# Two more MLP pairs by seven products, other low parts by adding transfers, and a new place for the scaled activations in a two-layer decoder trunk

## The chip, the cores and the metric

The kernel runs on one core of a Trainium2 chip. The metric is the device time of one execution in microseconds. Three runs of the kernel before took 1472.92, 1473.97 and 1474.12 us (median 1473.97). The engines are named as in the profile: PE is TensorE's matmul, PEld its weight load, DVE is VectorE, ACT is ScalarE, POOL is GpSimd, SP is SyncE, which here only issues transfers.

## The reference

A hybrid decoder trunk of two layers on one sequence of 512 positions with 1024 features, all float32. Layer 0 mixes with a gated short convolution and differential attention, layer 1 with stick-breaking attention. Each layer then attends into 256 memory tokens and applies a gated MLP of width 2816 with a causal convolution of width 3:

```python
def conv_ffn(h, w_up, w_conv, w_down):
    u = causal_dwconv(h @ w_up, w_conv)
    gate, val = jnp.split(u, 2, axis=-1)
    return (jax.nn.silu(gate) * val) @ w_down

for l in range(DEPTH):
    ...
    x = x + conv_ffn(rmsnorm(x, norm_ffn[l]), ffn_w_up[l], ffn_conv[l], ffn_w_down[l])
```

The change touches these two MLPs: `h @ w_up`, which has 1024 x 5632 weights in each layer.

## The kernel before

**Number format.** Every operand of a matmul is carried as two parts, a rounded one (`hi`) and the rest (`lo`), and every product is three matmuls: hi by hi, hi by lo, lo by hi. ScalarE casts the high part of a weight tile, VectorE subtracts it from the tile to get the low part (`lo<-raw,hi` in the profile). Weights come in tiles of 128 x 1024 (`raw`), by SP's queue, into three buffers; there are five buffers each for high and low parts.

**The up projection in pairs.** The 44 blocks of 128 output columns are worked on as 22 pairs, a gate block and its value block; the order of pairs and of the down projection's groups is the list `FFN_ORDER`. Pair j's weights are the group `Uj_l` of layer l. A pair is computed in one of two ways.

*Ordinary* (`lin_stream`): eight blocks of the contraction by two output blocks by three matmuls, 48 matmuls of 512 columns, two accumulators out of three. Pairs below `UP_SCALED` multiply by the activations before the normalization's factor per position (`N["A"]`, only the gains are in), and the factor is applied when the accumulator is evicted (`c<-acc,rrow`). Pairs from `UP_SCALED` on use scaled activations (`N["S"]`).

*Seven products* (`lin_halved`): the pair's matrix product is cut into two by two blocks (the two output blocks, even and odd blocks of the contraction, and the two halves of the positions) and made from seven products of blocks instead of eight. Each is 4 blocks x 3 matmuls of 256 columns, 84 in all. It needs sums of blocks on both sides. On the activations' side these are made once per MLP by `fold` out of the scaled activations, with their high and low parts (`N["S"]`, `N["T"]`, in tiles `y`, `h`, `kl`, `pt`, `so`, `rrow`), and no product of such a pair starts before `N["folded"]` allows. The results are put together by a copy and seven additions of 256 columns on ScalarE and VectorE.

On the weights' side the sums are made in DRAM (`sums_in_dram`): once the group named in `SUMMED` has produced its first output, SP's queue copies the four blocks (1 MB), and POOL's queue issues three adding transfers, one of 512 KB and two of 256 KB, each waiting for the one before it. `halved_loads` then loads three tiles of 1024 columns ("a", "b", "c") and one of 512 ("d"); each is cast on ScalarE and subtracted on VectorE.

**Low parts by an adding transfer.** For groups in `LOW`, VectorE does nothing. ScalarE writes the negated high part into the low tile, and an adding transfer of 512 KB, issued by POOL, adds the weights from DRAM:

```python
yield act(hi, raw)
if gi in LOW:
    yield act(lo, raw, scale=-1.0)
    yield add_dma(lo, wts[FIRST[gi] + s])
else:
    yield tt(lo, raw, hi.v().f32(), ALU.subtract)
```

**What sets the order.** The whole program is written out in advance by a planner (`Issue.run`). Every piece of work is a stream that asks for one operation at a time; the planner knows a cost for each, takes the engine whose next operation could start first, and among those that could start within a small tolerance takes the lowest priority number. The engines then work through their queues in that order. The numbers that matter: norm chunks 0.5, norm sums `SUM`, the sums of seven products 0.9, evictions 1.0, attention's blocks from 2.0 on, preparing weights 3.0, and additions in DRAM 6.0. `fold` has the priority `FOLD`. Where two streams of the same engine are ready, a smaller number goes first; a stream that waits on another engine is passed.

**Places.** Work buffers of 512 columns (`c`) are six; `fold` uses two for each of its four steps, an eviction one until its convolution is done. The lines that the profile names are helpers: L439 and L442 ScalarE copies and activations, L454 two-tensor operations on VectorE, L462 its three-operand ones (convolution, scaling), L492 matmuls, L501 transfers by SP, L508 adding transfers by POOL. The normalization's row of factors is the tile `rrow`.

Of the kernel before, what the change touches and what calls it, by code (L numbers as in the profile page):

```python
# [34 lines left out]

UP_SCALED = 6
FFN_ORDER = [('u', 0), ('u', 1), ('u', 2), ('u', 3), ('u', 4), ('u', 5), ('u', 6), ('u', 7), ('d', 0, 0), ('u', 8), ('d', 0, 1), ('u', 9), ('u', 10), ('d', 0, 2), ('u', 11), ('u', 12), ('d', 0, 3), ('u', 13), ('u', 14), ('u', 15), ('u', 16), ('d', 1, 0), ('u', 17), ('d', 1, 1), ('u', 18), ('d', 1, 2), ('u', 19), ('u', 20), ('d', 1, 3), ('u', 21), ('d', 2, 0), ('d', 2, 1)]
SEVEN = {0: (7, 8, 9, 10, 11, 12, 13, 14, 15, 16, 17, 18, 19, 20, 21), 1: (7, 8, 9, 10, 11, 12, 13, 14, 15, 16, 17, 18, 19, 20, 21)}  # L40

SUMMED = {0: {7: 'A1', 8: 'A1', 9: 'A2', 10: 'A2', 11: 'EO0', 12: 'EO0', 13: 'EO1', 14: 'KV1_0', 15: 'KV3_0', 16: 'Q0_0', 17: 'Q0_0', 18: 'Q1_0', 19: 'XO0_0', 20: 'XO0_0', 21: 'XO1_0'}, 1: {7: 'U17_0', 8: 'U19_0', 9: 'U21_0', 10: 'SQK0', 11: 'SQK0', 12: 'SV0', 13: 'SQK1', 14: 'SQK2', 15: 'SV1', 16: 'SQK3', 17: 'Q0_1', 18: 'Q1_1', 19: 'XO0_1', 20: 'XO1_1', 21: 'U1_1'}}


def weight_groups():
# [57 lines left out]
GROUPS = weight_groups()  # L103
GN = {g[0]: i for i, g in enumerate(GROUPS)}

LOW = {GN[n] for n in ('U2_0', 'U2_1', 'U3_0', 'U3_1', 'U4_0', 'U4_1', 'U5_0', 'U5_1', 'U6_0', 'U6_1')}
LOW7 = {GN[n] for n in ()}
ADDED = {GN[f"U{j}_{l}"]: GN[after] for l in SUMMED for j, after in SUMMED[l].items()}
HALVED = {GN[f"U{j}_{l}"] for l in SEVEN for j in SEVEN[l]}
NSLOT = [len(g[3]) * len(g[4]) * P // SLOT for g in GROUPS]  # L110
# [37 lines left out]

POW_WAIT = 0.0

PREP_FIRST, SUM_FIRST, SUM = 0.45, 3.2, 1.5

FOLD = 1.4

SUMS = 6.0
PE_RATE, PE_FIX = 2400.0, 0.0133
# [88 lines left out]
class Issue:  # L245
# [8 lines left out]
    def spawn(self, gen, prio):  # L254
        self.seq += 1
        self.streams.append(Stream(gen, prio, self.seq))
# [75 lines left out]
    @staticmethod  # L332
    def free(*ts):
        for t in ts:
            t.pool.idle.append(max(max(w + LAT.get(e, 0.0) for w, e in t.w), max(t.r)))
# [54 lines left out]
def trunk(ctx: ExitStack, tc: tile.TileContext, xT: bass.AP, memT: bass.AP, wts: bass.AP, par: bass.AP, outT: bass.AP):  # L390
# [36 lines left out]
    def act(out, in_, func=AF.Copy, scale=1.0, bias=None, accum=None):  # L427
        out, in_ = vw(out), vw(in_)
        scale, bias, accum = vw(scale), vw(bias), vw(accum)
        d = (0.051 if in_.psum() else 0.093) + in_.n() / 1200.0  # L430
        d += 0.093 * (isinstance(scale, V) + (bias is not None)) + 0.2 * (accum is not None)
        kw = {}
        if bias is not None:
            kw["bias"] = _raw(bias)
        if accum is not None:
            kw["accum_out"] = _raw(accum)
        if func == AF.Copy and scale is not None and not isinstance(scale, V) and scale == 1.0:
            def fn():
                return nc.scalar.copy(out=out.ap, in_=in_.ap)  # L439
        else:  # L440
            def fn():
                return nc.scalar.activation(out=out.ap, in_=in_.ap, func=func, scale=_raw(scale), **kw)  # L442
        return Op("ACT", d, [in_, scale, bias], [out, accum], fn)
# [299 lines left out]
    def prep(groups):  # L743
        for gi in groups:
# [3 lines left out]
            for s in range(NSLOT[gi]):  # L748
# [9 lines left out]
                else:  # L758
                    yield Until(lambda: (gi, s) in raws)
                    raw = raws[gi, s]  # L760
# [3 lines that stand above are left out]
# [114 lines left out]
    def lin(name, kind, A, done, nblk=None):  # L878
        gi = GN[name]
        c = len(GROUPS[gi][4]) * P  # L880
        nm_ = len(GROUPS[gi][4]) if kind == "f" else nblk
        for ki in range(len(GROUPS[gi][3])):
            for m in range(nm_):
                s = (ki * c + (m * P if kind == "f" else 0)) // SLOT
                uses[gi, s] = uses.get((gi, s), 0) + 1
        for m in range(nm_):
            ps = yield AL(aSC if (name, m) in (("V", 3), ("QK0", 0)) else aACC)
            lin_seq[0] += 1
            spawn(lin_stream(gi, m, kind, A, ps, done, c), 10.0 + lin_seq[0] * 1e-3)

    def lin_done(*names):

        def f():
            for n in names:
                gi = GN[n]
                if fin.get(gi, 0) < nm_of[n]:
                    return False
            return True
        return Until(f)
# [80 lines left out]
    def hs_free(N):  # L980
        for h, l in N["A"].values():
            free(h, l)
# [480 lines left out]
    def ffn(l, xin, xout, last):  # L1463
# [40 lines left out]
        def up_done(j):  # L1504
            def done(m, ps):
                gate = m % 2 == 0
                u = ps
                if j < UP_SCALED:
                    u = yield AL(pC)
                    yield Until(lambda: "rrow" in N)  # L1510
                    yield tt(u, ps, N["rrow"], ALU.mult)
                    free(ps)
                t = yield AL(pG)
                yield from conv3(u, f"ffn_conv{l}", j if gate else 22 + j, 44, t)
                free(u)
                if gate:
                    yield act(t, t, AF.Silu)
                    gate_t[j] = t
                    F["silu", l] = F.get(("silu", l), 0) + 1
                else:  # L1520
                    yield Until(lambda: j in gate_t)
                    yield tt(t, t, gate_t[j], ALU.mult)
                    free(gate_t[j])
                    if 4 <= j < 16 or j > 19:
                        q = pHS if j < 16 else pG
                        hi, lo = yield [AL(q, F32R), AL(q, F32R)]
                        o, w = (hi, lo), (hi, lo)
                    else:
                        y = yield AL(pH, F32R, (P, 2, S))
                        o, w = (y[:, 0, :], y[:, 1, :]), (y,)  # L1530
                    yield from split(o[0], o[1], t)
                    free(t)
                    own[j] = w
                    acts[j] = o
            return done

        def up(j):
            done = up_done(j)
            if j in SEVEN[l]:
                acc = yield AL(aACC)  # L1540
# [3 lines left out]
            scaled = Lazy(lambda k: N.get("S", {}).get(k))  # L1544
            yield from lin(f"U{j}_{l}", "f", scaled if j >= UP_SCALED else N["A"], done)

# [29 lines left out]
        def nfree():  # L1576
            yield lin_done(*(f"U{j}_{l}" for j in range(UP_SCALED)))
            hs_free(N)
            yield lin_done(*(f"U{j}_{l}" for j in range(UP_SCALED, 22)))
            free(*N["own"])  # L1580
            yield Until(lambda: 21 in acts)
            free(N["r"], N["rrow"])
        spawn(nfree(), 0.1)

        spawn(fold(), FOLD)
        for step in FFN_ORDER:
# [283 lines left out]
```

## Time and profile before

| | us |
|---|---|
| median of three runs | 1473.97 |
| the profiled execution | 1473.73 |
| its span | 1471.9 |
| TensorE busy | 1465.0 |
| VectorE busy | 1113.1 |
| ScalarE busy | 810.7 |
| POOL busy | 168.5 |

The granted clock was 1.0. The span is about: 0 to 345 the first mixer and memory attention, up to 375 its output projection, 375 to 690 the first MLP, 690 to 861 stick-breaking attention, up to 1120 its output projection and the second memory attention, then the second MLP to the end.

How to read the rows: of a row of instructions in order of time the first number is its start from the span's begin, the second its length, both in us; "out<-in" are the program's tiles; in brackets stands how long the engine had been idle before it and what ended that. A matmul's length is longer than its distance to the next, since matmuls are pipelined. A group row has the count behind x, then busy us, mean ns of one, and idle time before them.

### The profile page before, as it was taken

To read this page: it belongs to the slowest core of one execution; us is meant where nothing else is said; L and a number is where in the kernel's file an instruction comes from. 1 tells how busy PE (TensorE), PEld (TensorE's weight loads), DVE (VectorE), ACT (ScalarE), POOL (GpSimd) and SP (SyncE) were. 2 spreads that over 40 slices of the span, in tenths; PEclk is the share of its full clock that TensorE was granted. 3 is DMA by queue.
4 is the path that set the end of the run, shared out by engine and by line. 5 is a ranking of instruction groups with operands and counts; after the bars stand their busy time and mean duration, and the time that the engine had idled before them with its cause. 6 is when DMAs were issued, how large, how long until landed. Compare 5 with 4: busy or idle time off the path is not lost.

```text
span 1471.9 us, 21459 instructions
## 1 busy us (share of the span) xinstructions
PE 1465.0 (100%) x8048; PEld 1272.2 (86%) x8048; DVE 1113.1 (76%) x1891; ACT 810.7 (55%) x1335; POOL 168.5 (11%) x249
## 2 busy tenths in 40 slices
PE   9999999999999999999999999999999999999998
PEld 8888888888889999999888888888888889999897
DVE  7689766665798788867687989967656996888683
ACT  6576546453675445444477877855535854545341
POOL 3212121211210000000111111001101300000000
PEclk9999999999999999999999999999999999999999
DMA  6128898967784445658465463453547954455351
GB/s 237 58 86 243 224 264 269 255 169 161 178 177 143 144 151 170 200 169 227 158 154 147 122 187 79 137 178 107 148 126 219 224 149 128 144 159 184 117 165 57
DMA packets 86088, 243.41 MB, mean 165 GB/s; under 512 B 8064, under 2 KB 8576, under 8 KB 85504
## 3 DMA queue, kind: packets, MB, share of 16 engines
q1 hardware_dynamic: 63744, 200.09, 40.2%
q0 software_dynamic: 22240, 41.95, 17.6%
q8 instruction: 63, 1.03, 0.3%
q14 instruction: 41, 0.34, 0.1%
HBM read 239.91 MB, written 65.01 MB: 207 GB/s over the span
## 4 chain that ended last, share of the span: by engine, by line
PE 95%; DVE 2%; ACT 2%; DMA 1%; issue 1%; SPq 0%; DVEq 0%; ACTq 0%
PE acc L492 67%; PE sc L492 13%; PE pv L492 6%; PE tr L492 6%; PE tr L496 3%; DVE lo L454 0%; ACT h L439 0%; DMA raw<-wts 0%; ACT g L442 0%; DMA x<-xT 0%; DVE g L1619 0%; DVE h L454 0%; DVE g L454 0%; DVE c L454 0%; ACT pt L439 0%
## 5 line engine op out<-in xcount | busy, mean ns | idle before, releaser
L492 PE MATMUL acc<-hs,hi 128*128 128x512 f32 x1568 | 493.7, 392 | 0.0
L439 ACT CAST hi<-raw 128x1024 fp32r<-128x1024 f32 (+1 forms) x294 | 303.3, 1038 | 211.1 <-PE acc L492 79.8
L454 DVE TENSOR_TENSOR lo<-raw,hi 128x1024 fp32r<-128x1024 f32 (+1 forms) x274 | 328.7, 1205 | 90.7 <-ACT hi L439 89.5
L492 PEld LDWEIGHTS acc<-hs,hi 128*128 128x128 f32 x1568 | 292.4, 188 | 57.7
L492 PE MATMUL acc<-hs,lo 128*128 128x512 f32 x784 | 307.5, 392 | 0.0
L492 PE MATMUL acc<-hi,hs 128*128 128x512 f32 x544 | 175.4, 395 | 0.3 <-ACT hs L442 0.3
L492 PEld LDWEIGHTS acc<-hs,lo 128*128 128x128 f32 x784 | 147.3, 188 | 28.7
L492 PE MATMUL acc<-h,hi 128*128 128x512 f32 (+1 forms) x600 | 170.2, 368 | 0.0
L454 DVE TENSOR_TENSOR x<-x,acc 128x512 f32<-128x512 f32 (+1 forms) x105 | 71.2, 680 | 71.4 <-PE acc L492 71.1
L492 PEld LDWEIGHTS acc<-h,hi 128*128 128x128 f32 x600 | 108.2, 189 | 18.1
L462 DVE SCALAR_TENSOR_TENSOR g<-c,pp,g 128x511 f32<-128x511 f32 (+1 forms) x168 | 116.9, 745 | 2.5 <-ACT g L442 2.4
L492 PEld LDWEIGHTS acc<-hi,hs 128*128 128x128 f32 x544 | 100.9, 188 | 20.3 <-ACT hs L442 0.6
L492 PE MATMUL acc<-h,lo 128*128 128x512 f32 (+1 forms) x300 | 109.5, 368 | 0.0
L492 PE MATMUL acc<-lo,hs 128*128 128x512 f32 x272 | 106.8, 393 | 0.0
L492 PE MATMUL acc<-y,hi 128*128 128x512 f32 (+1 forms) x280 | 74.2, 346 | 0.0
L508 POOL DMA_DIRECT2D dr<-wts x30 | 27.4, 913 | 392.1 <-DMA dr<-wts 385.6
L442 ACT ACTIVATE g<-c,pp 128x512 f32<-128x512 f32 x84 | 58.1, 719 | 19.1 <-DVE c L454 18.9
L454 DVE TENSOR_TENSOR g<-g,g 128x512 f32<-128x512 f32 (+2 forms) x112 | 62.9, 568 | 5.0 <-ACT g L439 2.0
L492 PEld LDWEIGHTS acc<-h,lo 128*128 128x128 f32 x300 | 56.6, 189 | 9.4
L442 ACT ACTIVATE g<-sc,rq 128x128 f32<-128x128 f32 (+7 forms) x128 | 61.2, 537 | 5.4 <-PE sc L492 4.9
L508 POOL DMA_DIRECT2D dr<-dr x60 | 50.3, 848 | 115.3 <-DMA dr<-wts 70.1
L492 PEld LDWEIGHTS acc<-lo,hs 128*128 128x128 f32 x272 | 51.2, 188 | 10.0
(241 smaller groups left out, 2672.1 us busy)
## 6 DMA issues: line engine op xcount, KB each, us to landing
raw<-wts SPq DMA_DIRECT2D x226, 512.0 KB, 4.2
raw<-dr SPq DMA_DIRECT2D x60, 512.0 KB, 3.7
dr<-wts POOLq DMA_DIRECT2D x30, 512.0 KB, 6.1
dr<-dr POOLq DMA_DIRECT2D x60, 256.0 KB, 4.7
lo<-wts POOLq DMA_DIRECT2D x20, 512.0 KB, 7.8
raw<-wts SPq DMA_DIRECT2D x38, 256.0 KB, 3.1
x<-xT SPq DMA_DIRECT2D x16, 256.0 KB, 4.7
raw<-memT SPq DMA_DIRECT2D x4, 512.0 KB, 4.5
```

Of the source, the lines that this page charges most:

```text
L439: return nc.scalar.copy(out=out.ap, in_=in_.ap)
L442: return nc.scalar.activation(out=out.ap, in_=in_.ap, func=func, scale=_raw(scale), **kw)
L454: lambda: _ve(eng).tensor_tensor(out=out.ap, in0=in0.ap, in1=in1.ap, op=op))
L462: lambda: nc.vector.scalar_tensor_tensor(out=out.ap, in0=in0.ap, scalar=_raw(scalar), in1=in1.ap, op0=op0, op1=op1))
L492: lambda: nc.tensor.matmul(out.ap, lhsT.ap, rhs.ap, start=start, stop=stop))
L496: return Op("PE", 0.109, [in_, ident_v], [out], lambda: nc.tensor.transpose(out.ap, in_.ap, ident_v.ap))
L508: lambda: nc.gpsimd.dma_start(out=out.ap, in_=i, accum_op=ALU.add, max_dma_last_dim=2048))
```

## The change

Pairs 5 and 6 of both MLPs go from ordinary to seven products, and pair 5 no longer gets the factor at eviction, since it uses the scaled activations. The groups with low parts by an adding transfer were pairs 2 to 6 and are pairs 1 to 4. The additions in DRAM are 34 instead of 30, and the groups after which they are made are new: in layer 0 most come earlier by one or two groups and four come after pairs 7 to 10 of the MLP itself; ten of layer 1's come during layer 0's MLP, none in stick-breaking attention's projections, and four after pairs 8 to 11 of layer 1's MLP. `fold` gets priority 0.8, which is ahead of evictions (1.0) instead of behind them, and the norm sums 0.7 instead of 1.5.

```diff
-UP_SCALED = 6
+UP_SCALED = 5
-SEVEN = {0: (7, 8, 9, 10, 11, 12, 13, 14, 15, 16, 17, 18, 19, 20, 21), 1: (7, 8, 9, 10, 11, 12, 13, 14, 15, 16, 17, 18, 19, 20, 21)}
-
-SUMMED = {0: {7: 'A1', 8: 'A1', 9: 'A2', 10: 'A2', 11: 'EO0', 12: 'EO0', 13: 'EO1', 14: 'KV1_0', 15: 'KV3_0', 16: 'Q0_0', 17: 'Q0_0', 18: 'Q1_0', 19: 'XO0_0', 20: 'XO0_0', 21: 'XO1_0'}, 1: {7: 'U17_0', 8: 'U19_0', 9: 'U21_0', 10: 'SQK0', 11: 'SQK0', 12: 'SV0', 13: 'SQK1', 14: 'SQK2', 15: 'SV1', 16: 'SQK3', 17: 'Q0_1', 18: 'Q1_1', 19: 'XO0_1', 20: 'XO1_1', 21: 'U1_1'}}
+SEVEN = {0: (5, 6, 7, 8, 9, 10, 11, 12, 13, 14, 15, 16, 17, 18, 19, 20, 21), 1: (5, 6, 7, 8, 9, 10, 11, 12, 13, 14, 15, 16, 17, 18, 19, 20, 21)}
+
+SUMMED = {0: {5: 'A0', 6: 'A1', 7: 'A1', 8: 'A2', 9: 'A2', 10: 'EO0', 11: 'EO0', 12: 'EO1', 13: 'KV1_0', 14: 'Q0_0', 15: 'Q0_0', 16: 'Q1_0', 17: 'XO0_0', 18: 'U7_0', 19: 'U8_0', 20: 'U9_0', 21: 'U10_0'}, 1: {5: 'U9_0', 6: 'U11_0', 7: 'U12_0', 8: 'U13_0', 9: 'U14_0', 10: 'U15_0', 11: 'U16_0', 12: 'U17_0', 13: 'U18_0', 14: 'U20_0', 15: 'Q0_1', 16: 'Q1_1', 17: 'XO0_1', 18: 'U8_1', 19: 'U9_1', 20: 'U10_1', 21: 'U11_1'}}
...
-LOW = {GN[n] for n in ('U2_0', 'U2_1', 'U3_0', 'U3_1', 'U4_0', 'U4_1', 'U5_0', 'U5_1', 'U6_0', 'U6_1')}
+LOW = {GN[n] for n in ('U1_0', 'U1_1', 'U2_0', 'U2_1', 'U3_0', 'U3_1', 'U4_0', 'U4_1')}
...
-PREP_FIRST, SUM_FIRST, SUM = 0.45, 3.2, 1.5
-
-FOLD = 1.4
+PREP_FIRST, SUM_FIRST, SUM = 0.45, 3.2, 0.7
+
+FOLD = 0.8
```

## The prediction

> **What bounds the kernel now.** I read the page first: busy times, then the chain that ended last.
>
> ```profile
> span 1471.9 us, 21459 instructions
> PE 1465.0 (100%) x8048; PEld 1272.2 (86%) x8048; DVE 1113.1 (76%) x1891; ACT 810.7 (55%) x1335; POOL 168.5 (11%) x249
> ...
> PE 95%; DVE 2%; ACT 2%; DMA 1%; issue 1%; SPq 0%; DVEq 0%; ACTq 0%
> ```
>
> TensorE holds 95% of the chain: fewer or shorter matmuls are worth their full time, as long as nothing makes TensorE wait. Next the chain in order of time, which shows TensorE's pace in the gated MLP, and windows (columns: PE, PEld, DVE, ACT and POOL busy with counts, granted clock, DMA share, GB/s) over the first MLP's start, its rest, three seven-product pairs in a row, and the stick-breaking layer.
>
> ```profile
> 461.50 12.34 PE acc L492 x60
> 473.84 1.44 PE sc L492 x12
> ...
> 389.50:452.00 62.50, 62.50 (x281) 51.85 (x280) 58.19 (x95) 44.99 (x63) 8.42 (x7) 1.00 0.77 177
> 452.00:690.00 238.00, 238.00 (x1642) 222.80 (x1641) 185.05 (x282) 111.31 (x149) 5.09 (x6) 1.00 0.56 173
> 560.00:590.00 30.00, 30.00 (x252) 30.00 (x251) 28.66 (x48) 18.63 (x26) 0.00 (x0) 1.00 0.58 180
> 690.00:861.00 171.00, 169.99 (x840) 141.50 (x839) 141.23 (x228) 118.86 (x224) 28.14 (x76) 1.00 0.57 151
> ```
>
> In the MLP TensorE never stops. VectorE is the engine behind it: 58.19 of 62.50 us (93%) in the first seven pairs, when the scaled activations are made, and 28.66 of 30 (96%) over three seven-product pairs in a row, still without a TensorE gap.
>
> **The gain on TensorE.** Twelve 256-column matmuls take 1.44 us, 0.120 each, so a seven-product pair (7 x 4 x 3 = 84) takes 10.08 us. The x60 piece is 48 matmuls of 512 columns and the first twelve of the next pair: 12.34 - 1.44 = 10.90 us for 48, which is also what an ordinary pair has (8 x 2 x 3). One pair converted saves 0.82 us. Pairs 5 and 6 of two MLPs are four: -3.28 us.
>
> A rule of the Trainium skill speaks against this (TensorE: Matmul & The Clock Gate, "Back-to-back issue gap"): in a stream of weight loads and matmuls it gives 131 ns a matmul at 512 columns and 81 at 128. An estimate between the two by columns is 98 ns at 256: 8.2 us for the 84 against 6.3 for the 48, a loss of 1.9 per pair and 7.8 in all. The rows decide: 0.120 and 0.227 here.
>
> **What moves onto VectorE, and when.** Four moments in the first MLP (groups over 389.4 to 452, then instructions in order of time):
>
> ```profile
> L462 DVE SCALAR_TENSOR_TENSOR g<-c,pp,g 128x511 f32<-128x511 f32 (+1 forms) x24 | 17.5, 744 | 1.2 <-ACT g L442 1.2
> L454 DVE TENSOR_TENSOR c<-acc,rrow 128x512 f32<-128x512 f32 x12 | 8.1, 685 | 5.0 <-ACT rrow L439 3.6 <-PE acc L492 1.5
> L454 DVE TENSOR_TENSOR c<-c,c 128x256 f32<-128x256 f32 x8 | 3.3, 418 | 0.0
> ...
> 389.49 1.29 DVE L454 TENSOR_TENSOR c<-acc,rrow 128x512 f32<-128x512 f32 x2 [3.55 <-ACT rrow L439]
> 390.70 0.74 DVE L462 SCALAR_TENSOR_TENSOR c<-x,pp,rrow 128x512 f32<-128x512 f32 x1
> ...
> 431.11 1.22 DVE L454 TENSOR_TENSOR lo<-raw,hi 128x1024 fp32r<-128x1024 f32 x1
> 432.24 0.75 DVE L462 SCALAR_TENSOR_TENSOR g<-c,pp,g 128x511 f32<-128x511 f32 x1
> 432.91 0.68 DVE L454 TENSOR_TENSOR pt<-c,pt 128x512 fp32r<-128x512 f32 x1
> ...
> 449.68 0.68 DVE L454 TENSOR_TENSOR rrow<-c,pt 128x512 fp32r<-128x512 f32 x1
> 450.28 1.22 DVE L454 TENSOR_TENSOR lo<-raw,hi 128x1024 fp32r<-128x1024 f32 x1
> ...
> 451.27 0.40 PE L492 MATMUL acc<-y,hi 128*128 128x256 f32 x2
> ```
>
> At 389.5 the row of norm factors exists and VectorE's rush begins. The last part of the scaled activations ends at 450.3, and pair 7, the first of seven products, starts at 451.27: just in time. Starts one after another give what an operation occupies: 0.60 us for 512 columns (two in 1.21), 0.67 for the convolution's (432.24 to 432.91), 1.13 for a low part of 1024; 0.42 stands for 256. So the scaled activations take 8 x 0.67 + 16 x 0.60 + 16 x 0.42 = 21.7 us; evicting an ordinary scaled pair 2 x (0.60 + 2 x 0.67) + 2 x 0.60 = 5.1; the weights of a seven-product pair 3 x 1.13 + 0.60 = 4.0.
>
> Pair 0 started 7 x 10.90 us before 451.27, at 375.0, so pair 5 is due at 429.5. Its sixth product, which wants its last weights, is due 5 x 1.44 = 7.2 us later, at 436.7. Before, the same point of pair 7 is at 458.5: 69.0 us after 389.5, for 21.7 + 6 x 5.1 + 3.9 (pair 6, unscaled, 5.1 - 1.2) + 4.0 = 60.2 us of work; 9 us spare. After: 47.2 us for 21.7 + 5 x 5.1 + 4.0 = 51.2. Four us too much, if every eviction of pairs 0 to 4 must come before pair 5's weights. None needs to: TensorE wants their buffers, which the first 0.60 us of each half frees. What must be done by 436.7 is 21.7 + 4.0 + 10 x 0.60 and enough convolutions that the six work buffers don't run out. But the weights have the lowest claim on VectorE (3.0 against 1.0 for evictions); they pass only where no eviction is ready. The low part at 431.11 is such a passing, with the scaled activations (1.4) still unfinished. At 429.5 the backlog is 21.7 + 25.5 - 40.0 = 7.2 us, with some 2.5 halves under way, each often waiting for ScalarE. I take no stall (they pass), and as bounds 0 and strictly last: 7.2 + 1.1 = 8.3 us per MLP.
>
> That the scaled activations come first has a price at 389.5: their first two operations (1.34 us) go ahead of the eviction that frees an accumulator for pair 1's second half, due at 375.0 + 3 x 5.45 = 391.35. The eviction would end at 389.5 + 1.34 + 0.6 = 391.4, and the signal comes on top: 0.2 us per MLP, +0.4 (bounds 0 and 2 x 1.3).
>
> **Low parts by adding transfer.** Pairs 5 and 6 had theirs from the transfer and get them from VectorE (counted above). Pair 1 goes the other way: VectorE loses 2 x 1.13 us before 389.5, where it is no limit, and ScalarE gains two passes of 1.04. But the transfer has to land.
>
> ```profile
> 374.23 1.04 ACT L439 CAST hi<-raw 128x1024 fp32r<-128x1024 f32 x1
> 375.17 0.63 ACT L442 ACTIVATE sq<-x 128x512 f32<-128x512 f32 x1
> ...
> 376.49 1.22 DVE L454 TENSOR_TENSOR lo<-raw,hi 128x1024 fp32r<-128x1024 f32 x1
> ...
> 381.04 1.24 POOL L508 DMA_DIRECT2D lo<-wts  x1 [10.56 <-DVE nacc L454]
> ...
> DMA to landing us min/median/max: 6.3/8.9/10.6
> ...
> DMA to landing us min/median/max: 7.3/8.8/11.8
> ```
>
> Pair 1's first weights are cast at 374.23. Behind a square (0.63) the negated copy ends near 376.8, the add is issued near 377.0 and lands, at the median (8.9 in the window 375 to 400, 8.8 at 1120 to 1145), at 385.9. TensorE first wants it at 375.0 + 10.9 + 0.45 = 386.35. Cover 0.4 us; I take 0, with bounds 0 and 2 x (377.0 + 11.8 - 386.35) = 4.9. In POOL's queue the adds stand ahead of the power that gives the norm's factors (each 1.24), a delay inside the cover of three waiting accumulators.
>
> **The other moves cost nothing I can see.** Norm sums at 0.7 instead of 1.5 now pass evictions (1.0), but already passed weights (3.0), and they wait for the chunks that those evictions make; bounds -0.6 and +0.6, one operation. Four more pairs are added up in DRAM and most additions move out of the stick-breaking layer into the MLPs:
>
> ```profile
> q1 hardware_dynamic: 63744, 200.09, 40.2%
> q0 software_dynamic: 22240, 41.95, 17.6%
> ...
> 769.95 6.26 DMA raw<-wts
> ...
> raw<-wts SPq DMA_DIRECT2D x226, 512.0 KB, 4.2
> ```
>
> The queues' shares of 1471.9 us give 2.96 us of all 16 engines per MB of copies and 6.2 per MB of adds; one addition (1.05 MB each) is 9.6 us. It leaves a layer whose only weight load on the chain took 6.26 us instead of 4.2, and whose TensorE is idle 1.0 us of 171 by the window above. I take -0.4 (bounds 0 and -1.0).
>
> **Sum.** The profiled execution took 1473.73 us, 1.8 around its span; it lies 0.24 below the median of 1473.97, which I leave alone. 1473.73 - 3.28 + 0.4 - 0.4 = 1470.45; half the 0.24 back gives **1470.6 us**.
>
> **Rivals.**
> *Weights partly late.* Pair 5's first weights pass at about 431.5, not 429.5: 2 us per MLP, 1474.6. For it: on paper VectorE is 4.0 us short, and it runs at 93% even now. Against: it ran at 96% at 560 to 590 with no gap on TensorE.
> *Weights strictly last (slower than before).* With the scaled activations first, all evictions of pairs 0 to 4 pile up into one stretch, several halves are always ready, and pair 5's low parts wait for the end of the backlog: 8.3 us per MLP, 1470.6 + 16.6 = 1487.2. It decides from 1.7 us per MLP on, and past 0.2% from 3.2. Against: the passing at 431.11.
> *Pair 1's add lands late.* At the longest landing 4.9 us, 1475.5; it would hide as much of any later wait.
> *Transfers crowd the first MLP.* Fourteen additions instead of three: 11 x 9.6 = 106 us more over the 238, so the share goes from 0.56 to 1.0. Their 1 MB copies stand in SP's queue between the weights' loads, which could come late, as at 769.95; POOL's queue has nothing behind them (5.09 us busy of 238).
> At 1 us of TensorE each, 11 make 1481.6. Against: this window ran at 1.04 with TensorE full:
>
> ```profile
> 1145.00:1155.00 10.00, 10.00 (x46) 8.28 (x45) 9.09 (x17) 8.45 (x13) 3.96 (x4) 1.00 1.04 232
> ```
>
> The Trainium skill (DMA: Bandwidth & Descriptors, "Queues, rings and completion order") says each engine takes turns between queues, packet by packet; no run here shows the turns themselves.
> *The weight loads bind.* PEld is busy 30.00 of 30 at 560 to 590. Were the new pairs spaced by their loads at 10.90 / 84 = 0.130 us instead of 0.120, nothing would be gained: 1473.9. Against: 1.44 per twelve everywhere, also where three such pairs follow each other. By the rule of the Trainium skill's page on TensorE, cited above, it would be 7.8 more, 1481.7.
>
> **How the numbers follow.** Forecast 0.45, partly late 0.24, strictly last 0.17, pair 1's add 0.06, crowded transfers 0.07, loads bind 0.01. About 0.2% (2.9 us) is what a measurement of this kernel can tell from no change: faster means below 1471.0. Of the forecast's 0.45, 0.42 lies there. Faster 0.42; same 0.03 + 0.24 + 0.06 + 0.01 - 0.01 (its tail) = 0.33; slower 0.17 + 0.07 + 0.01 = 0.25. The range goes from 1468.8 (0.4 + 0.6 + 0.6 by the bounds that gain, 0.2 for scatter) to 1481 (5.2 us per MLP).
>
> **What would show it.** Right: pair 5 starts about 54.5 us after pair 0, in both MLPs; the scaled activations end before 425; 336 more matmuls of 256 columns and 192 fewer of 512. Wrong: TensorE waiting for VectorE's low part at pair 5 or 6, for POOL's add at pair 1, or for weights landing late between 460 and 670; VectorE below 95% from 389 to 437 with TensorE waiting would mean that order, not load, is the cause.

## The result, and the profile after

The changed kernel takes 1494.07 us (median of four runs, 1490.83 to 1497.23) against 1473.47 for the kernel before beside it (1472.92 to 1474.12): ratio 1.014, with a 95% interval of 1.0114 to 1.0165. It is 20.6 us slower. The prediction was 1470.6 us, with a range up to 1481.0, and faster as the likeliest sign; it is wrong in both.

The profiled execution took 1492.35 us. Its page, busy times and the chain that ended last by engine:

```profile
span 1490.4 us, 21827 instructions
PE 1468.0 (98%) x8192; PEld 1279.3 (86%) x8192; DVE 1127.0 (76%) x1927; ACT 815.7 (55%) x1343; POOL 172.9 (12%) x257
...
PE 80%; DMA 8%; DVE 7%; ACT 3%; issue 1%; SPq 0%; DVEq 0%; ACTq 0%
```

TensorE's part of the chain falls from 95% to 80%, and DMA, VectorE and ScalarE take it over, DMA first (1% to 8%). The work itself is what was meant: 8192 matmuls are 144 more than 8048, as 336 of 256 columns more and 192 of 512 fewer make. Where TensorE stands still is read from windows over the first MLP's start, its rest, and the 40 us in which it is worst (columns as in the prediction: PE, PEld, DVE, ACT, POOL busy, granted clock, DMA share, GB/s):

```profile
389.50:452.00 62.50, 61.11 (x348) 53.94 (x349) 61.77 (x105) 41.01 (x60) 4.79 (x4) 1.00 0.60 153
452.00:706.00 254.00, 242.25 (x1647) 224.97 (x1646) 189.74 (x292) 115.45 (x154) 35.56 (x42) 0.99 0.91 262
590.00:630.00 40.00, 33.79 (x237) 31.49 (x236) 28.04 (x44) 18.42 (x24) 7.54 (x9) 1.00 1.05 294
```

In the rest of the first MLP TensorE is idle 11.75 of 254 us, where before it was idle 0.00 of 238; the DMA share there is 0.91 instead of 0.56, and 1.05 where it is worst. The waits of TensorE in the whole span (us in total, times, longest; neither row is among those of before), and then those of ScalarE's casts for arriving weights, after and before:

```profile
PE sc L492 <- DVE c L454: 13.4, 8, 3.3
PE acc L492 <- DVE c L454: 3.2, 2, 2.0
```

```profile
ACT hi L439 <- DMA raw<-wts: 74.5, 51, 5.1
ACT hi L439 <- DMA raw<-dr: 60.4, 27, 4.4
```

```profile
ACT hi L439 <- DMA raw<-wts: 56.2, 34, 4.9
ACT hi L439 <- DMA raw<-dr: 19.7, 9, 3.6
```

By name TensorE waits for VectorE's additions and evictions (`c`), 16.6 us in ten waits. But upstream of it, the casts wait 60.4 instead of 19.7 us for the tiles of summed weights (`raw<-dr`). How the one becomes the other shows in the instructions in order of time around the longest wait:

```profile
592.96 1.05 ACT L439 CAST hi<-raw 128x1024 fp32r<-128x1024 f32 x1 [4.14 <-DMA raw<-dr]
...
594.04 1.23 DVE L454 TENSOR_TENSOR lo<-raw,hi 128x1024 fp32r<-128x1024 f32 x1 [3.42 <-ACT hi L439]
...
596.12 1.22 DVE L454 TENSOR_TENSOR lo<-raw,hi 128x1024 fp32r<-128x1024 f32 x1
597.25 0.42 DVE L454 TENSOR_TENSOR c<-c,sc 128x256 f32<-128x256 f32 x1
...
597.58 0.42 DVE L454 TENSOR_TENSOR c<-sc,c 128x256 f32<-128x256 f32 x1
...
598.05 0.50 PE L492 MATMUL sc<-y,hi 128*128 128x256 f32 x2 [3.35 <-DVE c L454]
```

A tile of weights lands late, ScalarE's cast has stood 4.14 us for it, and VectorE's low part 3.42 us for the cast. VectorE works through its queue in the written order, so the additions that put the previous pair's products together, whose inputs have long been there, stand behind this low part and the next one (596.12). The last row of VectorE frees the accumulator that TensorE wants next: it ends at 598.00, and TensorE goes on at 598.05. The chain of waits at the same place goes one step further back (start, length, what):

```profile
582.43 1.22 DVE lo L454
583.65 0.03 DVE c L454
583.68 9.26 DMA raw<-dr
```

It is a loop of one `raw` buffer: load, cast, low part, and only then is the buffer free for the next load (the low part of 582.43 ends at 583.65, and the load is issued at 583.68). With 9.26 us for the load this turn takes 11.6, from 583.65 to the end of the low part above (594.04 + 1.23).

### The profile page after: what moved, and what is told of

It is laid out like the page before. It is cut to its first block, busy times and chain, and to the rows that moved or that the text cites. A ratio compares the mean times of both kernels' runs of the same rounds, so it can differ in the third digit from the quotient of the medians.

```text
span 1490.4 us, 21827 instructions
## 1 busy us (share of the span) xinstructions
PE 1468.0 (98%) x8192; PEld 1279.3 (86%) x8192; DVE 1127.0 (76%) x1927; ACT 815.7 (55%) x1343; POOL 172.9 (12%) x257
## 3 DMA queue, kind: packets, MB, share of 16 engines
q8 instruction: 64, 1.05, 0.3%
## 4 chain that ended last, share of the span: by engine, by line
PE 80%; DMA 8%; DVE 7%; ACT 3%; issue 1%; SPq 0%; DVEq 0%; ACTq 0%
PE acc L492 56%; PE sc L492 11%; PE pv L492 5%; PE tr L492 5%; DMA raw<-wts 4%; DMA raw<-dr 3%; PE tr L496 3%; DVE lo L454 2%; DVE c L454 1%; ACT hi L439 1%; DVE g L462 1%; DVE h L454 1%; DVE c L462 1%; ACT h L439 0%; ACT lo L442 0%
## 5 line engine op out<-in xcount | busy, mean ns | idle before, releaser
L492 PE MATMUL acc<-hs,hi 128*128 128x512 f32 x1504 | 477.8, 393 | 3.2 <-DVE c L454 3.2
L454 DVE TENSOR_TENSOR lo<-raw,hi 128x1024 fp32r<-128x1024 f32 (+1 forms) x282 | 338.7, 1206 | 109.9 <-ACT hi L439 108.1
L492 PEld LDWEIGHTS acc<-hs,hi 128*128 128x128 f32 x1504 | 282.2, 189 | 59.7 <-DVE c L454 4.0
L492 PE MATMUL acc<-hs,lo 128*128 128x512 f32 x752 | 296.1, 394 | 0.0
L492 PEld LDWEIGHTS acc<-hs,lo 128*128 128x128 f32 x752 | 142.0, 189 | 27.5
L492 PE MATMUL acc<-h,hi 128*128 128x512 f32 (+1 forms) x584 | 163.5, 365 | 0.0
L462 DVE SCALAR_TENSOR_TENSOR g<-c,pp,g 128x510 f32<-128x510 f32 (+1 forms) x176 | 122.6, 746 | 0.0
L508 POOL DMA_DIRECT2D dr<-dr x68 | 61.0, 906 | 159.3 <-DMA dr<-wts 109.4
L492 PE MATMUL acc<-y,hi 128*128 128x256 f32 (+1 forms) x264 | 67.3, 338 | 0.0
L492 PE MATMUL sc<-y,hi 128*128 128x256 f32 x272 | 52.8, 286 | 13.4 <-DVE c L454 13.4
```

Source lines behind the costliest of these rows:

```text
L454: lambda: _ve(eng).tensor_tensor(out=out.ap, in0=in0.ap, in1=in1.ap, op=op))
L462: lambda: nc.vector.scalar_tensor_tensor(out=out.ap, in0=in0.ap, scalar=_raw(scalar), in1=in1.ap, op0=op0, op1=op1))
L492: lambda: nc.tensor.matmul(out.ap, lhsT.ap, rhs.ap, start=start, stop=stop))
L508: lambda: nc.gpsimd.dma_start(out=out.ap, in_=i, accum_op=ALU.add, max_dma_last_dim=2048))
```

## The experiments

Each was compared with the kernel before on the same chip (medians there 1473.75 to 1473.87). Intervals are 95%. The theory after the first look: the ten additions of layer 1 that the change put inside the first MLP crowd its loads. The rivals: VectorE's load and order at pairs 5 and 6, and the low parts of pair 1.

**Layer 1's ten additions back at such places as before.** Seven of the ten leave the first MLP; three stay in it, near its end, after pairs 17, 19 and 21. Edit against the changed kernel:

```diff
-1: {5: 'U9_0', 6: 'U11_0', 7: 'U12_0', 8: 'U13_0', 9: 'U14_0', 10: 'U15_0', 11: 'U16_0', 12: 'U17_0', 13: 'U18_0', 14: 'U20_0', ...
+1: {5: 'U17_0', 6: 'U19_0', 7: 'U21_0', 8: 'SQK0', 9: 'SQK0', 10: 'SV0', 11: 'SQK1', 12: 'SQK2', 13: 'SV1', 14: 'SQK3', ...
```

> The changed kernel with one thing undone: the ten additions of layer 1's pairs 5 to 14 go back to the places that such additions had before (three late in layer 0's MLP, seven in stick-breaking attention), so the first MLP holds seven additions instead of fourteen. Theory of crowded transfers: the waits between 520 and 640 us, 15 us of TensorE, mostly go; 1479 to 1483 against 1494. Theory of VectorE's order (evictions ahead of weights): nothing changes, 1492 to 1495.

Measured: 1479.86 us, 1.004 (1.0025 to 1.0054); 14.2 us come back. The window over the rest of the first MLP:

```profile
452.00:706.00 254.00, 251.57 (x1700) 233.43 (x1699) 197.54 (x303) 119.45 (x160) 16.34 (x20) 1.00 0.71 207
```

TensorE idles 2.4 us there instead of 11.75, at a DMA share of 0.71 instead of 0.91. The places of these additions are the main part of the loss: 14.2 of 20.6 us, for ten additions moved, of which seven left this MLP.

**The places alone.** The kernel before, with nothing changed but that pairs 7 to 21 get their additions where the changed kernel has them:

```diff
-SUMMED = {0: {7: 'A1', 8: 'A1', 9: 'A2', ...}, 1: {7: 'U17_0', 8: 'U19_0', 9: 'U21_0', 10: 'SQK0', ...}}
+SUMMED = {0: {7: 'A1', 8: 'A2', 9: 'A2', ...}, 1: {7: 'U12_0', 8: 'U13_0', 9: 'U14_0', 10: 'U15_0', ...}}
```

> The kernel before with one thing of the change alone: the additions of pairs 7 to 21 of both layers at the changed places (ten or so of layer 1 and four of layer 0 during the first MLP); pairs 5 and 6 stay ordinary, all priorities and low parts as before. Theory of crowded transfers: slower than before by 6 to 14 us, with TensorE waiting between 520 and 640. Theory of VectorE's order: no change, 1473 to 1475.

Measured: 1480.68 us, 1.0049 (1.0034 to 1.0064). The window, and the wait of TensorE that is new:

```profile
452.00:706.00 254.00, 248.15 (x1682) 230.70 (x1681) 190.80 (x291) 115.81 (x155) 30.51 (x36) 1.00 0.85 245
```

```profile
PE sc L492 <- DVE c L454: 5.8, 3, 3.1
```

6.9 us are lost with no other part of the change present, by the same wait. It is half of the 14.2. This run moves layer 0's additions too, which the first experiment leaves where they are; the changed kernel has two more of layer 1's in this MLP, and pairs 5 and 6 load faster than ordinary pairs; that these make the rest is argued, not shown.

**Copies without adding transfers.** The changed kernel; of layer 1's pairs 5 to 14 only the 1 MB copy is made, so their sums are missing and their loads read the bare copy:

```diff
 yield dma(d.v(), x, 2 * SLOT)
+if gi in {GN[f"U{j}_1"] for j in range(5, 15)}:
+    summed[gi] = d
+    return
 yield add_dma(d[0:2], x[1:3])
```

> The changed kernel, in which the ten layer 1 additions that come during the first MLP make only their 1 MB copy on SP's queue and leave out the three adding transfers on POOL's queue, so that the sums of these pairs are not made (their loads read the copy). If the adding transfers are what slows the weights' loads (6.4 of 9.6 us of engine time per addition), most of the 14 us that the first experiment won come back: 1480 to 1485. If the copies between the loads on SP's own queue are: 1490 or more.

Measured: 1481.63 us, 1.0049 (1.0034 to 1.0064).

```profile
452.00:706.00 254.00, 251.12 (x1701) 233.42 (x1700) 198.02 (x304) 120.58 (x160) 10.23 (x12) 1.00 0.70 226
```

The ten copies stay in SP's queue, which I had named as what stands between the loads, and 12.4 us come back all the same. It is the adding transfers: 30 of them carry 0.21 of the share (0.91 to 0.70). What the copies cost by themselves is not measured. In the first experiment this window has seven copies fewer and eight adding transfers more, and TensorE and the share come out alike (251.57 us, 0.71). Whether they hurt by the share alone or by something of their own in the transfer engines, no run here tells apart.

**Pair 1's low parts back on VectorE.** Edit: `U1_0` and `U1_1` out of `LOW`.

> The changed kernel with pair 1's low parts made by VectorE again instead of the adding transfer. Theory that pair 1's transfer (and the order that was written for it) causes the gaps at 388.9 and 1149.4: they go, 1.4 + 2.3 us and the slow clock behind the second, 4 to 6 us less, 1488 to 1490. Theory that these gaps come from the scaled activations ahead of the first eviction: they stay, 1493 to 1495.

Measured: 1495.21 us, 1.0144 (1.0123 to 1.0166). The waits went as the first theory said, but the 4 to 6 us did not come back. TensorE's wait for an eviction at pair 1 (the `acc` row) is gone, and another is there (waits, then VectorE and TensorE in order of time):

```profile
PE pv L492 <- DVE sq L454: 2.9, 2, 1.5
```

```profile
426.77 1.22 DVE L454 TENSOR_TENSOR lo<-raw,hi 128x1024 fp32r<-128x1024 f32 x1
...
429.57 0.40 PE L492 MATMUL acc<-y,hi 128*128 128x256 f32 x2
...
433.56 0.69 DVE L454 TENSOR_TENSOR sq<-raw,sq 128x512 fp32r<-128x512 f32 x1
```

Pair 5 now starts at 429.57, when it was due, and its first low part has passed in time (426.77). But the third of its products wants the short tile "d", whose low part comes at 433.56. In the changed kernel VectorE has both low parts earlier:

```profile
415.25 1.23 DVE L454 TENSOR_TENSOR lo<-raw,hi 128x1024 fp32r<-128x1024 f32 x1
...
429.97 0.69 DVE L454 TENSOR_TENSOR sq<-raw,sq 128x512 fp32r<-128x512 f32 x1
```

There pair 5 starts at 430.89, and even from 429.57 on its third product, due two products later (2.88 us), would have found "d" ready at 430.66. So the wait at pair 1 did not hide this one: the edit made the planner write another order, and the new wait came with it.

**Both of the former.** The additions of the first and the low parts of this one together.

> Both of the others on the changed kernel: additions of layer 1 out of the first MLP, pair 1's low parts by VectorE. If crowded transfers and pair 1 explain everything, 1473 to 1477 and near the kernel before. If VectorE's order still costs something at pairs 5 and 6, TensorE waits there and it stays above 1480.

Measured: 1481.92 us, 1.0052 (1.0035 to 1.0069), 4.9 above the upper end of the first expectation; the second one, above 1480 with a wait at pair 5, came true.

```profile
PE sc L492 <- DVE c L454: 5.1, 4, 2.3
```

Besides pair 5's two waits (2.9 us, as in the experiment before) there are still waits of the first kind, the longest near 538 and 1287, where the change has four additions of layer 0 and four of layer 1 inside their own MLPs.

**No addition in the middle of an MLP.** The first experiment, and the four additions that each layer has inside its own MLP come earlier too, which moves some of the others: layer 0's pairs 14 to 21 follow the memory attention's groups, layer 1's 15 to 21 its output projection and the second memory attention:

```diff
-0: {... 13: 'KV1_0', 14: 'Q0_0', 15: 'Q0_0', 16: 'Q1_0', 17: 'XO0_0', 18: 'U7_0', 19: 'U8_0', 20: 'U9_0', 21: 'U10_0'}
+0: {... 13: 'KV1_0', 14: 'KV2_0', 15: 'KV3_0', 16: 'Q0_0', 17: 'Q0_0', 18: 'Q1_0', 19: 'Q1_0', 20: 'XO0_0', 21: 'XO0_0'}
-1: {... 15: 'Q0_1', 16: 'Q1_1', 17: 'XO0_1', 18: 'U8_1', 19: 'U9_1', 20: 'U10_1', 21: 'U11_1'}
+1: {... 15: 'SO0', 16: 'KV1_1', 17: 'KV3_1', 18: 'Q0_1', 19: 'Q1_1', 20: 'Q1_1', 21: 'XO0_1'}
```

> The changed kernel with all additions taken out of the middle of both MLPs (layer 0's end before the first MLP begins; layer 1's come three late in the first MLP, seven in the stick-breaking projections, seven in its output projection and the second memory attention). Theory of crowded transfers: no wait of TensorE is left after pair 6 of either MLP, and what remains against the sum of the prediction are the gaps at pair 1 (1.3 and 2.2 us with their slow clock): 1474 to 1477. If waits of 1 us or more remain at pairs 11 to 18, the additions are not the cause of all: above 1479.

Measured: 1480.25 us, 1.0041 (1.0026 to 1.0056), 3.2 above the expectation, so the additions are not the cause of all. The window, and the waits that are left:

```profile
452.00:706.00 254.00, 253.92 (x1723) 236.30 (x1722) 200.63 (x309) 121.76 (x162) 6.80 (x8) 1.00 0.59 177
```

```profile
PE acc L492 <- DVE c L454: 3.7, 2, 2.5
PE acc L492 <- ACT hi L439: 1.4, 1, 1.4
```

The first MLP is full again (253.92 of 254), at a share of 0.59. What is left is the wait at pair 1 and a new one of 1.4 us at 263, ahead of the first MLP, where a weight load is late and where the earlier additions now stand; three small waits in the MLPs make another 1.1. The median is no lower than the first experiment's 1479.86, so taking these eight out of the MLPs shows no gain in the time.

**Pair 5's and 6's weights ahead of evictions.** The former, pair 1's low parts on VectorE, and in `prep`:

```diff
+PREP[0].prio = 0.95 if GROUPS[gi][0][:3] in ('U5_', 'U6_') else 3.0
```

> As the one before, but pair 1's low parts by VectorE, and the weights of pairs 5 and 6 prepared with priority 0.95, ahead of evictions. Theory that VectorE's order makes the weights of pair 5 late: the wait of 1.6 us for their part d at pair 5 goes in both MLPs and TensorE has no gap at all in the MLPs: 1470 to 1472, faster than both kernels. If it is VectorE's load and not its order, the wait moves to another operation and it stays at 1474 or more.

Measured: 1477.93 us, 1.0027 (1.0017 to 1.0038). In the stretch of pairs 5 to 7:

```profile
425.00:458.00 33.00, 32.19 (x235) 30.22 (x234) 33.00 (x56) 19.35 (x30) 0.00 (x0) 1.00 0.42 120
```

It stays above 1474, as was expected if VectorE's load is the cause. VectorE has no idle time at all in 33 us, and TensorE still stands 0.8: in this stretch and order VectorE is the bound. That no better order exists is not shown.

**`fold` behind evictions again.** The additions out of the MLPs as two above, `FOLD` 1.4 and `SUM` 1.5 as before.

> As the first of these four, but with the scaled activations behind evictions again (1.4) and the norm sums at 1.5, as before. If the new place of the scaled activations is needed for pair 5, they end later than pair 5 is due (431) and TensorE waits up to 10 us per MLP: 1485 to 1495. If evictions first would have done as well: the same as the first of these, within 2 us.

Measured: 1495.66 us, 1.0145 (1.0129 to 1.016); 15.4 slower than with `fold` first. TensorE's wait in it, once in each MLP:

```profile
PE acc L492 <- DVE lo L454: 13.3, 2, 6.9
```

That the scaled activations come first is needed if pair 5 is to use them. The wait for an eviction at pair 1 is down to 0.2 us here, so it needs `fold` ahead of the eviction (or the norm sums, which this run moved back as well).

**Relieving VectorE by adding transfers.** The same as with the weights ahead; layer 0's additions back where the kernel before had them, pairs 5 and 6 both after `A0`; and the low parts of the tiles "b" and "c" of pairs 5 and 6 by adding transfers:

```diff
-LOW7 = {GN[n] for n in ()}
+LOW7 = {GN[n] for n in ('U5_0', 'U5_1', 'U6_0', 'U6_1')}
```

> As the kernel with the weights of pairs 5 and 6 ahead of evictions and all additions out of the MLPs, but layer 0's additions stand where they stood before (pairs 5 and 6 after A0), and two of the three large tiles of pairs 5 and 6 get their low parts by the adding transfer instead of VectorE, which takes 2 x 2.27 us off VectorE per MLP. If VectorE's load around 425 to 455 is what is left (waits of 0.2, 0.85 and 0.2 us per MLP), they go, the waits at 263 and 297 go too, and it comes to 1470 to 1473. If the adding transfers are late, TensorE waits for them at pair 5 or 6 and it stays at 1475 or more.

Measured: 1485.53 us, 1.0085 (1.0071 to 1.0099). The chain at TensorE's longest wait (4.8 us, in the first MLP; one as long in the second):

```profile
442.57 6.95 DMA raw<-dr
```

A load of summed weights again, 6.95 us, and TensorE stops within pair 6. Pair 6's own adding transfers are issued just before (437.51 and 439.92); the next experiment leaves them out. The written order is another too (two products of pair 7 stand inside pair 6's), so which of the two makes the wait is not told apart.

**The same for pair 5 alone.** `LOW7` holds `U5_0` and `U5_1`.

> The same with the adding transfer for pair 5 alone. By VectorE's load: waits of 0.85 us or less per MLP remain at pair 6, 1471 to 1475. If the transfers of pair 6 are the late ones, it is better than the one before it.

Measured: **1472.03 us** (ten runs, 1470.25 to 1473.45), ratio **0.9986** (0.9977 to 0.9995): faster than both, than the kernel before by 0.14%. Its page and its windows:

```profile
span 1468.5 us, 21822 instructions
PE 1462.0 (100%) x8192; PEld 1276.7 (87%) x8192; DVE 1126.9 (77%) x1927; ACT 813.3 (55%) x1343; POOL 173.6 (12%) x257
```

```profile
389.50:452.00 62.50, 62.50 (x364) 55.57 (x363) 60.79 (x106) 42.86 (x64) 5.99 (x5) 1.00 0.69 174
452.00:690.00 238.00, 238.00 (x1637) 222.52 (x1636) 190.15 (x292) 115.94 (x153) 5.10 (x6) 1.00 0.57 178
```

All 8192 matmuls of the change are there, and TensorE is full through the first MLP; no wait is left at pair 6. The span is 3.4 us below 1471.9. That profiled execution (1470.25) was the fastest of the ten; in the medians the gain is 1.8.

**From pair 6 on only.** The kernel before with pair 6 by seven products, pair 5 left ordinary, `fold` first; `LOW` pairs 2 to 5, one more addition per layer, the others unmoved.

> The kernel before with pair 6 alone added to the seven products (pair 5 ordinary with its factor at eviction), the scaled activations at 0.8, additions as before plus two, low parts by adding transfer for pairs 2 to 5. TensorE saves 2 x 0.82 = 1.64 us. By the account of VectorE's time there are 58 us for 56 us of work ahead of pair 6's last weights, so waits of at most 1 us per MLP: 1472 to 1474. If the place of the scaled activations by itself makes TensorE wait: 1476 or more.

Measured: 1472.58 us, 0.9995 (0.9986 to 1.0003): not told apart from no change. 1.64 us were to be had; the profiled span of 1470.9 shows 1.0.

## Why the prediction was wrong

**The step that failed** is "The other moves cost nothing I can see", with its -0.4 us, and behind it the argument "Against: this window ran at 1.04 with TensorE full", which left the crowding of the first MLP at 0.07. The size of the traffic was worked out right: I had 0.56 rising to 1.0, it is 0.91, and 1.05 at the worst. As a rival ("Transfers crowd the first MLP") it had the late loads and a price near the truth, 11 us for 11 additions against the 13.8 that come back when all eleven leave (1480.25, in a run that clears layer 1's MLP as well); but "1 us of TensorE each" had no row behind it, so its nearness is luck. It also named the wrong half: the copies in SP's queue, where the adding transfers, with "nothing behind them" in POOL's queue, make the loads late. What was wrong is the row that I set against it. In 1145 to 1155 TensorE was full, but I read only TensorE and the share there, not the landing. Landing of the loads of `raw`, in us (min, median, max): first before in that window, then before, after and in the first experiment from 452 to 690:

```profile
DMA to landing us min/median/max: 6.8/6.8/6.9
```

```profile
DMA to landing us min/median/max: 2.4/3.7/7.4
```

```profile
DMA to landing us min/median/max: 3.2/5.3/12.0
```

```profile
DMA to landing us min/median/max: 2.6/4.2/10.3
```

So in that window the loads (two of them) were slow already, 6.8 against 3.7; the pair just did not mind. An ordinary pair loads 2 tiles in 10.90 us, a tile in 5.45, so each of three buffers has 16.35 us for a turn. A seven-product pair loads four tiles in 10.08 us, one in 2.52, since the short one takes a whole buffer too (`AL(pRAW, F32, (P, w), ...)` takes one of the three at any width), and a buffer has 7.56. Cast (1.05) and low part (1.22) come off that: 5.3 us are left for the landing. The median of 3.7 fits, one of 5.3 with a tail to 12.0 doesn't, and the turn of 11.6 in the chain above is such a tail. The runs line up with it: at medians of 3.7 (before), 4.2 (first experiment), 5.0 (the places alone) and 5.3 us (the change) TensorE is idle 0.0, 2.4, 5.9 and 11.75 us in the rest of the first MLP. The budget is an estimate from rows for pairs that follow one another; a fourth buffer, which would test it by itself, wasn't tried. The prediction took slack for insensitivity: it moved a proof from pairs with 14 us of cover to pairs with 5.

**TensorE's gain, -3.28: right.** The version with pair 5's low parts by transfer has a TensorE 3.0 us less busy (1462.0 against 1465.0) and a span 3.4 shorter. In medians 1.8 of it arrives. "The weight loads bind" is refuted by the same run.

**First eviction behind `fold`, +0.4 with a bound of 2.6: the right mechanism, mis-sized; the bound was exceeded.** Two waits make 3.2 us, and the second is followed by 3 us at half clock (below), about 1.5 more. The eviction came 1.34 us after the row of factors, as in the working, and even earlier than foretold, at 389.68, since the row came at 388.34 instead of 389.49. But TensorE wanted the accumulator at 389.1, not at 391.35:

```profile
388.34 1.42 DVE L462 SCALAR_TENSOR_TENSOR c<-x,pp,rrow 128x512 f32<-128x512 f32 x2 [4.35 <-ACT rrow L439]
...
389.68 0.68 DVE L454 TENSOR_TENSOR c<-acc,rrow 128x512 f32<-128x512 f32 x1
...
390.41 0.73 PE L492 MATMUL acc<-hs,hi 128*128 128x512 f32 x2 [1.17 <-DVE c L454]
```

In TensorE's written order four matmuls of pair 1's second half now stand ahead of the last ten of its first half. The likely reason, argued and not tried by itself, is that the planner counts 10 us for an adding transfer to land, and so put something else first. With pair 1's low parts on VectorE the order is the old one and the wait is gone; with `fold` behind the evictions it is gone too. So it takes both edits, and I had costed each by itself. That half clock follows the second wait was no term of mine.

**Pair 1's adding transfer, 0: right as far as it goes.** TensorE never waited for it. But it has a part in the wait just told, through the order that the planner writes when it reckons with the transfer.

**Weights of pair 5, no stall: right in the changed kernel**, whose rows have no wait of TensorE for them. With pair 1's low parts on VectorE it is 1.5 us per MLP, about the size of "partly late". There it is not the first weights, which passed ahead of the scaled activations' last part as I said they would, but the short tile "d", which I had not followed: of a pair's four tiles I took the due time of the last (the sixth product), and in that order the third product's tile is the one that binds. "Strictly last" did not happen.

**Norm sums, +-0.6:** the page shows no wait for them; nothing more is known. **Additions out of stick-breaking attention, -0.4:** the window 706 to 861 has TensorE busy 154.65 of 155.00, idle 0.35 against the 1.0 from 690 to 861 before, so it is about the size foretold.

The profiled span is 21.8 us above 1471.9 - 3.28. TensorE's two new kinds of wait are 16.6, the two stretches at half clock about 2.8 by estimate. The waits count from the modelled ends of matmuls; the remaining 2.4 us, over ten restarts, I cannot resolve further.

Of the signs named, "weights landing late between 460 and 670" came true; pair 5 began 55.9 us after pair 0 instead of 54.5, and the scaled activations ended at 427.5 instead of before 425. VectorE was at 99% (61.77 of 62.50) from 389.5 on, so there it was load.

## What to carry to other kernels

Before a transfer is moved into a stretch because "the share is below 1", work out what one buffer's turn may take there (buffers times the pitch of the tiles, a short tile counting as a whole one, less what the engines do with one), and compare it with the landing at the share that will be. A stretch that stays full at a high share proves only that its own slack is enough; look at the landing in it, not at the engine that is full. And an edit that takes a wait away can make the planner write another order, with another wait in it: take it away in an experiment before its whole length is counted as a gain.

## What the runs showed of the hardware that was not expected

After a wait of 2.0 us TensorE's clock fell to half for at least 3.0 us, after one of 2.9 (up to 629.36) it did as well, and after one of 3.35 it didn't. Windows of the changed kernel over the longest and the shortest of the three and what follows, and over what follows the middle one (the number before the last two is the granted clock):

```profile
594.40:598.00 3.60, 0.31 (x3) 0.10 (x1) 3.60 (x7) 1.43 (x3) 0.00 (x0) 1.00 1.11 240
598.00:602.00 4.00, 3.94 (x33) 3.95 (x34) 3.84 (x7) 3.32 (x5) 0.81 (x1) 1.00 1.04 422
1149.30:1151.80 2.50, 0.48 (x4) 0.06 (x2) 2.09 (x4) 1.64 (x4) 0.04 (x1) 1.00 1.08 295
...
1152.90:1155.90 3.00, 3.00 (x8) 2.34 (x7) 3.00 (x8) 1.35 (x2) 0.08 (x1) 0.50 1.08 283
...
630.80:633.40 2.60, 2.60 (x9) 2.12 (x9) 2.07 (x6) 0.29 (x1) 0.00 (x0) 0.50 1.62 675
```

In the window from 1152.90 on, seven matmuls of 512 columns start, 0.43 us apart, where 13 fit at 0.227. The half clock sets in about a microsecond after the work has started again, and among these waits it isn't the length that decides. The Trainium skill (TensorE: Matmul & The Clock Gate, "Part 1: The HAM clock gate") has an activity window of about 3.4 us that runs freely, which would fit both the 3 us and the missing tie to length; its advice in "Why this matters for your kernels", no idle gaps over about 3 us, is not safe by these rows, since 2.0 us were enough once.

The adding transfers are the dear part of an addition: 30 of them, half of the ten additions' bytes, raise the share in the first MLP from 0.70 to 0.91 and the median landing of its loads from 4.3 to 5.3 us.
